# One-core hybrid streaming step with expert retrieval: 88 instead of 72 score blocks ahead in layer 0, 94 instead of 82 in layer 1, the sample's second chain from block 40, own slots for the additions' index

## The chip, the cores and the metric

The kernel runs on one core of a Trainium2 chip. The metric is the device time of one execution in microseconds; lower is better. Three runs of the kernel before took 3999.14, 4004.71 and 4008.16 us, so the median is 4004.71 us. All times in the profile count from the start of its span.

## The reference

Two layers run over 512 prompt tokens (one stream) and 128 sample tokens (8 streams of 16) with shared weights and a model width of 1024. Layer 0's mixer is a gated convolution beside sliding-window attention, layer 1's is a gated linear recurrence in blocks of 16 tokens. After each mixer stands the expert retrieval, which is the bulk of the work:

```python
q = (xb @ w_query).reshape(TB, 8, 2, 128)            # 8 heads, two halves
s = einsum('thpd,hpkd->thpk', q, keys)               # 128 keys for each half
sv, si = top_k(s, 16)
cand = sv[:, :, 0, :, None] + sv[:, :, 1, None, :]   # 16 x 16 pairs
cv, ci = top_k(cand, 16);  gate = softmax(cv)        # 16 of 16384 experts a head
act = gelu(einsum('thkd,td->thk', u_tab[idx], xb))
y = einsum('thk,thkd->td', gate * act, v_tab[idx])   # u_tab, v_tab: 16384 x 1024
```

Everything is float32; the products are made of two float32r parts of each factor, so a product takes three matmuls.

## The kernel before, in words

Tokens are worked in tiles of 128: four of the prompt, one of the sample. The retrieval is done in two ways.

*By gathers* (`sparse_peer`, L852): for the sample's tile and the prompt's first tile, in both layers. For each of 128 chosen experts a token, POOL issues an indirect load of one row of `u` per token (512 KB, L880), the vector engine multiplies and sums it (L884); then 128 rows of `v` in the same way (L913, summed by L920; in layer 0 for the sample L944, summed on TensorE by L962). The six buffers `g` are shared, so a gather is issued when the vector engine is through with the sixth before it.

*Densely* (`dense_peer`, L974): the prompt's tiles 1 to 3 meet all 16384 experts, in 128 blocks of 128. A block takes a load of `uT`, its split in two parts by ScalarE (L240) and the vector engine (L241), 24 matmuls of scores, a gelu, a multiplication by the gates of that block (L1110), a second split, a load and split of `v`, and 18 matmuls into the accumulators (`combine`, L1122). The gates come from a table in DRAM (`gd`) that `found` builds tile by tile from one-hot products. In layer 1 the first of these tiles gets its gates otherwise: `spread` (L1052) adds each token's gates into a cleared table `gz` by 128 indirect DMAs, in groups of 16 with a fence (`stone`, L1063) between; the first fence also waits for the DMAs that clear `gz` (L180).

Scores don't need the gates. So the last NA of the 128 are scored ahead (`ahead`, L985): FIRST of them while the query projections run (`route_p`), EACH more in each step of `found`, the rest behind it. Their scores go to DRAM (`sd`, L997) and come back in the loop (`ge<-sd`). `FE = (FIRST, EACH, NA)` is (12, 5, 72) in layer 0 and (12, 8, 82) in layer 1. So the loop computes scores for the first 56 blocks in layer 0 and the first 46 in layer 1.

The sample's path is a chain of its own (`chain_s`): mixer, query projections, choice, and then its gathers, which are appended to the list `gathers`. Its layer 0 chain runs beside the prompt's mixer; its layer 1 chain is started within layer 0's dense loop at block `K0`, one step a block. `gather(n)` takes n steps of the first entry of `gathers`; the numbers GM, GR, GS and PACE say how many at each step of the mixer, the projections, the gates' stretch and the dense loop. In layer 0's loop it is called only if the first tile's gathers are at the head or the sample's chain isn't done.

The program text doesn't fix the order of the instructions. A scheduler of the tile framework orders each engine's list by priorities (the place in the text, plus 1000 for gathers in layer 0, in the mixers and in the gates' stretch) and by its own estimate of when operands are ready. Engines then run their lists strictly in that order, and SP and POOL issue their DMAs in theirs. `after` and `follow` add order-only edges.

Buffers: `ai` (5) holds the transposed choices of `found` and in layer 1 the index of `spread`; `gatea` (2) holds the gates of the dense tiles.

## Time and profile before

| | |
|---|---|
| Median of 3 runs | 4004.71 us |
| Profiled execution, its own time | 4018.61 us |
| Its span | 4016.7 us, mean granted clock 0.94 |
| TensorE busy (weight loads) | 3567.8 us, 89% (2921.1, 73%) |
| Vector engine busy | 3217.4 us, 80% |
| ScalarE, POOL busy | 1655.5 and 1596.2 us |
| DMA | 1097.66 MB, mean 273 GB/s |
| Largest shares of the chain of waits | L1122 on TensorE 10%, L1070 on POOL 5%, loads `ge<-sd` 4%, `gu<-u` 3% |

The stages, by the first and last instruction of each: mixer of layer 0 to about 420, query projections to 656, gates' stretch to 1116, dense loop 1116 to 2094, mixer of layer 1 to about 2620, projections and gates' stretch to 3271.7, dense loop to 4005. Busy shares are averages over these, and the stages have different limits; what a change in one of them is worth is read from that stage. PE is TensorE's matmuls, PEld its weight loads, DVE the vector engine, ACT ScalarE. The granted clock is a share of TensorE's upper level; a matmul at the lower level takes longer and so counts as more busy time.

### The profile page before, as it was taken

To read this page: it belongs to the slowest core of one execution; us is meant where nothing else is said; L and a number is where in the kernel's file an instruction comes from. 1 tells how busy PE (TensorE), PEld (TensorE's weight loads), DVE (VectorE), ACT (ScalarE), POOL (GpSimd) and SP (SyncE) were. 2 spreads that over 40 slices of the span, in tenths; PEclk is the share of its full clock that TensorE was granted. 3 is DMA by queue.
4 is the path that set the end of the run, shared out by engine and by line. 5 is a ranking of instruction groups with operands and counts; after the bars stand their busy time and mean duration, and the time that the engine had idled before them with its cause. 6 is when DMAs were issued, how large, how long until landed. Compare 5 with 4: busy or idle time off the path is not lost.

```text
span 4016.7 us, 51334 instructions
## 1 busy us (share of the span) xinstructions
PE 3567.8 (89%) x17676; PEld 2921.1 (73%) x17676; DVE 3217.4 (80%) x6206; ACT 1655.5 (41%) x2717; POOL 1596.2 (40%) x1173
## 2 busy tenths in 40 slices
PE   6978778999999999788998878787999949999998
PEld 4756666789779997556775555566999949998776
DVE  5558999886568879887679877899998738788898
ACT  6644222467633334334444333231348913333333
POOL 0001665431245555541003553564057764444443
PEclk8989899999999999999999777798999979999999
DMA  4334998886789999998665765688457769999999
GB/s 147 113 110 160 328 338 322 317 326 241 264 298 336 338 333 357 370 362 304 227 230 216 258 235 186 225 321 296 140 164 211 211 177 343 334 337 356 385 385 331
DMA packets 480134, 1097.66 MB, mean 273 GB/s; under 512 B 55537, under 2 KB 260337, under 8 KB 474737
## 3 DMA queue, kind: packets, MB, share of 16 engines
q1 hardware_dynamic: 313984, 557.38, 39.7%
q0 software_dynamic: 165888, 537.01, 37.9%
q8 instruction: 139, 2.28, 0.2%
q14 instruction: 123, 1.00, 0.1%
HBM read 1005.92 MB, written 89.23 MB: 273 GB/s over the span
## 4 chain that ended last, share of the span: by engine, by line
PE 22%; DVE 12%; DMA 10%; POOL 6%; issue 5%; ACT 1%; SPq 0%; DVEq 0%; POOLq 0%; ACTq 0%
PE py L1122 10%; POOL gz L1070 5%; DMA ge<-sd 4%; DMA gu<-u,idx 3%; PE ps L284 2%; DVE wlo L241 2%; DVE yv L920 2%; PE pb L284 2%; PE py L291 1%; PE py L292 1%; PE py L293 1%; DMA gz<-gatea,ati 1%; DVE gu L884 1%; PE ps L312 1%; DMA wraw<-v 1%
## 5 line engine op out<-in xcount | busy, mean ns | idle before, releaser
L240 ACT ACTIVATE whi<-wraw 128x1024 fp32r<-128x1024 f32 x710 | 741.3, 1054 | 1024.5 <-PE py L292 307.6
L241 DVE TENSOR_TENSOR wlo<-wraw,whi 128x1024 fp32r<-128x1024 f32 x710 | 862.0, 1217 | 315.1 <-ACT whi L240 124.9
L880 POOL DMA_INDIRECT gu<-u,idx x512 | 670.4, 1309 | 1028.5 <-DVE idx L874 380.1
L1122 PE MATMUL py<-whi,wt 128*128 128x512 f32 x3072 | 798.8, 405 | 107.4 <-ACT wt L240 90.6
L1122 PEld LDWEIGHTS py<-whi,wt 128*128 128x128 f32 x3072 | 581.5, 192 | 258.9 <-ACT wt L240 102.3
L913 POOL DMA_INDIRECT gv<-v,idx x384 | 522.0, 1359 | 540.6 <-DVE yv L920 357.0
L884 DVE CUSTOM_DVE_ANT_0 gu<-gu,xnn 128x1024 f32<-128x1024 f32 x512 | 616.2, 1218 | 58.2 <-DMA gu<-u,idx 57.0
L291 PE MATMUL py<-xhl,whi 128*128 128x512 f32 (+1 forms) x1344 | 522.5, 389 | 74.5 <-ACT xhl L240 30.8
L293 PE MATMUL py<-xhl,wlo 128*128 128x512 f32 (+1 forms) x1344 | 515.9, 385 | 26.6 <-DVE wlo L241 26.3
L292 PE MATMUL py<-xhl,whi 128*128 128x512 f32 (+1 forms) x1344 | 514.1, 382 | 11.1 <-DVE xhl L241 11.0
L920 DVE SCALAR_TENSOR_TENSOR yv<-gv,wact,yv 128x1024 f32<-128x1024 f32 x381 | 486.7, 1277 | 2.7
L1122 PE MATMUL py<-wlo,wt 128*128 128x512 f32 x1536 | 401.6, 393 | 0.7 <-DVE wlo L241 0.7
L291 PE MATMUL ps<-xhl,whi 128*128 128x384 f32 (+1 forms) x1120 | 387.2, 346 | 7.9 <-ACT sm L510 3.7
L293 PE MATMUL ps<-xhl,wlo 128*128 128x384 f32 (+1 forms) x1120 | 388.5, 347 | 3.6 <-DVE wlo L241 3.4
L292 PE MATMUL ps<-xhl,whi 128*128 128x384 f32 (+1 forms) x1120 | 385.1, 344 | 0.0
L291 PEld LDWEIGHTS py<-xhl,whi 128*128 128x128 f32 x1344 | 264.6, 197 | 133.7 <-ACT xhl L240 35.1
L1122 PEld LDWEIGHTS py<-wlo,wt 128*128 128x128 f32 x1536 | 288.6, 188 | 67.6 <-DVE wlo L241 1.3
L1070 POOL DMA_INDIRECT gz<-gatea,ati x128 | 249.2, 1947 | 202.6 <-DVE mr L771 162.1
L293 PEld LDWEIGHTS py<-xhl,wlo 128*128 128x128 f32 x1344 | 264.4, 197 | 84.9 <-DVE wlo L241 37.7
L292 PEld LDWEIGHTS py<-xhl,whi 128*128 128x128 f32 x1344 | 264.8, 197 | 46.8 <-DVE xhl L241 15.1
L944 POOL DMA_INDIRECT gv<-v,idt x128 | 151.7, 1185 | 324.5 <-PE pb L962 296.3
L291 PEld LDWEIGHTS ps<-xhl,whi 128*128 128x128 f32 x1120 | 213.9, 191 | 21.3 <-ACT ge L996 5.8
(444 smaller groups left out, 4947.0 us busy)
## 6 DMA issues: line engine op xcount, KB each, us to landing
wraw<-uT SPq DMA_DIRECT2D x256, 512.0 KB
wraw<-v SPq DMA_DIRECT2D x256, 512.0 KB
wraw<-w SPq DMA_DIRECT2D x98, 512.0 KB
gd<-st SPq DMA_DIRECT2D x40, 1024.0 KB
wraw<-wq SPq DMA_DIRECT2D x64, 512.0 KB
sd<-ge SPq DMA_DIRECT2D x154, 192.0 KB
gch<-gd SPq DMA_DIRECT2D x32, 768.0 KB
ge<-sd SPq DMA_DIRECT2D x114, 192.0 KB
```

The costliest lines, as they stand in the source:

```text
L240: S.activation(hi, src, AF.Copy)
L241: return V.tensor_tensor(lo, src, hi.bitcast(F32), op=OP.subtract)
L284: m = T.matmul(p, w[wv][:, k], xhl(xv, k), start=(k == 0 and xv == wv), stop=(k == 7 and wv == 1))
L291: T.matmul(p, w[0][:, k], xhl(0, k), start=(k == 0), stop=False)
L292: T.matmul(p, w[0][:, k], xhl(1, k), start=False, stop=False)
L293: T.matmul(p, w[1][:, k], xhl(0, k), start=False, stop=(k == 7))
L880: P.indirect_dma_start(out=rows[s], out_offset=None, in_=t["u"][l], in_offset=bass.IndirectOffsetOnAxis(ap=idx[:, s:s + 1], axis=0))
L884: d = V.tensor_tensor_reduce(out=g, in0=g, in1=xn, scale=1.0, scalar=0.0, op0=OP.mult, op1=OP.add, accum_out=w[:, s - LG:s - LG + 1])
L913: P.indirect_dma_start(out=rows[s], out_offset=None, in_=t["v"][l], in_offset=bass.IndirectOffsetOnAxis(ap=idx[:, s:s + 1], axis=0))
L920: d = V.scalar_tensor_tensor(y, rows[e], w[:, e:e + 1], y, op0=OP.mult, op1=OP.add)
L1070: d = P.indirect_dma_start(out=flat, out_offset=bass.IndirectOffsetOnAxis(ap=ati[:, j:j + 1], axis=0), in_=gate[:, j:j + 1], in_offset=Non ...
L1122: mult[1] = T.matmul(yp[a][hf], wt[:, wv, 128 * a:128 * a + 128], vh[vv][:, 512 * hf:512 * hf + 512], start=(k == 0 and wv == 0 and vv == ...
```

## The change

Layer 0: NA 72 to 88 and EACH 5 to 7 (with DEEP, the number of blocks at the start whose scores and weights alternate between two buffers, 54 to 38), the first tile's gathers are appended at step 6 of the gates' stretch (KQ) instead of at block 1 of the loop, the sample's layer 1 chain starts at block 40 instead of 56 (K0), and `gather` is called in the loop whenever there is anything to gather. Layer 1: NA 82 to 94 and EACH 8 to 10, and the step that contains `spread` is written ahead of the first tile's own choice (`sparse_peer`). Buffers: the index of `spread` gets slots of other tiles (`idf`, `bt`), `gatea` three buffers; the zero tile that clears `gz` is halved, so the clearing goes in pieces of 512 bytes instead of 1024.

```diff
--- before.py
+++ after.py
@@ -26,7 +26,7 @@
 KT = (1, 0)
 LATER = 1000
 ORDER = ('SSPSPSPSPSPPPPPPPPSPSPPPSPSPSPSS','SPPP'*50)
-K0, SN = 56, (1,)
+K0, SN = 40, (1,)
 PS = 1000
 SW2 = [('g', 'g', 'g')]
 SB2 = ['s']
@@ -40,13 +40,13 @@
 PO = (0, 1)
 PEO = (0, 1)
 LG = 4
-DEEP = (54, 126)
+DEEP = (38, 126)
 LW = (1000, 1000)
 RS = 0
 SUM = dict(s=(None, "xn"), t=("vm", "vm"))
-KQ = (-1, -1)
+KQ = (6, -1)
 SC = (0, 1)
-FE = ((12, 5, 72), (12, 8, 82))
+FE = ((12, 7, 88), (12, 10, 94))
 
 
 class Group:
@@ -71,7 +71,7 @@
 
     BUFS = {"u4": 2, "uh": 2, "lo": 2, "v4": 4, "vh": 2, "w3": 2, "ge": 2, "g8": 2,
             "nat": 2, "g": NG, "sq": 2, "at": 2, "ai": 5, "vm": 1, "bt": 2, "bi": 2, "el": 2, "els": 2, "ln": 1,
-            "gatea": 2, "mr": 1, "xa": 2, "xb": 4}
+            "gatea": 3, "mr": 1, "xa": 2, "xb": 4}
 
     def tl(tag, shape, dt=F32, name=None):
         return sb.tile(shape, dt, name=name or tag, tag=tag, bufs=BUFS.get(tag, 1))
@@ -166,7 +166,7 @@
                         op0=OP.is_ge, op1=OP.mult)
         V.tensor_tensor(place[:, 0:1], place[:, 0:1], place[:, 1:2], op=OP.add)
     gz = dr.tile([4, 128, 128, 32], F32, name="gz", tag="gz", bufs=1)
-    zero = con.tile([128, 256], F32, name="zero")
+    zero = con.tile([128, 128], F32, name="zero")
     stone = con.tile([1, 1], F32, name="stone")
     fills = []
 
@@ -175,9 +175,9 @@
         while mark[0] is None:
             yield 1
         after(V.memset(zero, 0.0))
-        flat = gz.rearrange("g p k t -> (g p k t)").rearrange("(p r c) -> p r c", p=128, c=256)
-        for i in range(0, 64, 16):
-            fills.append(Y.dma_start(flat[:, i:i + 16], zero[:, None].to_broadcast([128, 16, 256])))
+        flat = gz.rearrange("g p k t -> (g p k t)").rearrange("(p r c) -> p r c", p=128, c=128)
+        for i in range(0, 128, 32):
+            fills.append(Y.dma_start(flat[:, i:i + 32], zero[:, None].to_broadcast([128, 32, 128])))
             for _ in range(6):
                 yield 1
 
@@ -1052,10 +1052,10 @@
         def spread(k1, k2, gate):
 
 
-            at = tl("ai", [128, 128], name="at0")
+            at = tl("idf", [128, 128], name="at0")
             V.scalar_tensor_tensor(at, k2, 128.0, k1, op0=OP.mult, op1=OP.add)
             V.tensor_scalar(at, at, 32.0, place[:, 0:1], op0=OP.mult, op1=OP.add)
-            ati = tl("ai", [128, 128], I32, name="ati")
+            ati = tl("bt", [128, 128], I32, name="ati")
             V.tensor_copy(ati, at)
             flat = gz.rearrange("g p k (t o) -> (g p k t) o", o=1)
             last = fills
@@ -1246,11 +1246,14 @@
             if i < FE[l][0]:
                 next(de)
             gather(GR[l])
+        if SC[l]:
+            next(de)
+            gather(GS[l])
         spt = sparse_peer(GT, l, xt, sv[:, 0], si[:, 0], "v4", SUM["t"][l])
         next(spt)
         if KT[l] < 0:
             gathers.append(spt)
-        for i in range(12 - 4 * SC[l]):
+        for i in range(12 - 5 * SC[l]):
             next(de)
             if i == KQ[l]:
                 gathers.append(spt)
@@ -1263,9 +1266,9 @@
             tg["s"] = dict(w=[SW1], sq="sq", r="pa", v="pb", a="idf", x="pa")
             cs = chain_s(1)
         for k, _ in enumerate(de):
-            if k == KT[l]:
+            if k == KT[l] and KQ[l] < 0:
                 gathers.append(spt)
-            if l or gathers and (gathers[0] is spt or cs is not None):
+            if gathers:
                 gather(PACE[l][k % len(PACE[l])])
             if l == 0 and cs is not None and k >= K0:
                 if spt not in gathers:
```

Three places of the engines' lists.

The vector engine in layer 1's mixer, before, at the end of a unit's state updates. L652 is a state update, L884 a gather's multiply and sum (its second row reads the sum out):

```order
L675 MEMSET s_in 128x128
L652 SCALAR_TENSOR_TENSOR s_in<-s_in,el,ps 128x128 x2
L652 SCALAR_TENSOR_TENSOR s_in<-s_in,el,py_18163 128x128 x2
L652 SCALAR_TENSOR_TENSOR s_in<-s_in,el,py_18167 128x128
L884 ISA gu,wact<-gu,xnn 128x1024
L884 ISA wact 128x1
L652 SCALAR_TENSOR_TENSOR s_end<-s_in,el,py_18167 128x128
L884 ISA gu,wact<-gu,xnn 128x1024
L884 ISA wact 128x1
```

And now, some way further on in the same mixer (L920 is the sum over gathered rows of `v`):

```order
L920 SCALAR_TENSOR_TENSOR yv<-gv,wact,yv 128x1024
L652 SCALAR_TENSOR_TENSOR s_in<-s_in,el,ps 128x128
L920 SCALAR_TENSOR_TENSOR yv<-gv,wact,yv 128x1024
L652 SCALAR_TENSOR_TENSOR s_in<-s_in,el,ps 128x128
L920 SCALAR_TENSOR_TENSOR yv<-gv,wact,yv 128x1024
L652 SCALAR_TENSOR_TENSOR s_in<-s_in,el,py_18768 128x128
L920 SCALAR_TENSOR_TENSOR yv<-gv,wact,yv 128x1024
L652 SCALAR_TENSOR_TENSOR s_in<-s_in,el,py_18768 128x128
L920 SCALAR_TENSOR_TENSOR yv<-gv,wact,yv 128x1024
L652 SCALAR_TENSOR_TENSOR s_in<-s_in,el,py_18772 128x128
```

Before, two gather steps stood among six updates; now one stands between any two, and the sample's `v` gathers, which had stood in the mixer's end and in the projections, are here.

SP before, at the end of layer 1's gates' stretch. `wraw<-uT` loads a block's weights, `sd<-ge` stores its scores ahead, `gd<-st` stores gates, `gch` reads them back, from `gz` those that were added:

```order
L997 DMA sd<-ge 128x384
L272 DMA wraw<-uT 128x1024
L997 DMA sd<-ge 128x384
L272 DMA wraw<-uT 128x1024
L1049 DMA gd<-st_25503 128x2048
L1049 DMA gd<-st_25504 128x2048
L272 DMA wraw<-uT 128x1024
L1105 DMA gch<-gz 128x4x128
L1107 DMA gch<-gd 128x8x128
L272 DMA wraw<-v 128x1024
L1105 DMA gch<-gz 128x4x128
```

And now:

```order
L1049 DMA gd<-st_26027 128x2048
L1049 DMA gd<-st_26028 128x2048
L997 DMA sd<-ge 128x384
L272 DMA wraw<-uT 128x1024
L1105 DMA gch<-gz 128x4x128
L1107 DMA gch<-gd 128x8x128
L997 DMA sd<-ge 128x384
L1105 DMA gch<-gz 128x4x128
L272 DMA wraw<-uT 128x1024
L1107 DMA gch<-gd 128x8x128
L997 DMA sd<-ge 128x384
```

Before, all loads and stores of the blocks ahead stood in front of the first read from `gz`; now ten blocks' stores and their loads stand behind it.

The vector engine at the end of the program, before. L1149 adds the dense result to the tokens, L901 the gathered one:

```order
L1110 TENSOR_TENSOR ge<-ge,gch 128x384
L920 SCALAR_TENSOR_TENSOR yv<-gv,wact,yv 128x1024 x2
L241 TENSOR_TENSOR wlo<-wraw,whi 128x1024
L241 TENSOR_TENSOR wt<-ge,wt 128x384
L920 SCALAR_TENSOR_TENSOR yv<-gv,wact,yv 128x1024 x2
L241 TENSOR_TENSOR wlo<-wraw,whi 128x1024
L920 SCALAR_TENSOR_TENSOR yv<-gv,wact,yv 128x1024 x4
L901 TENSOR_TENSOR xp<-xp,pb 128x4x128
L1149 TENSOR_TENSOR xp<-xp,py_32293 128x4x128
L1149 TENSOR_TENSOR xp<-xp,py_32302 128x4x128
L901 TENSOR_TENSOR xp<-xp,pb 128x4x128
```

And now:

```order
L920 SCALAR_TENSOR_TENSOR yv<-gv,wact,yv 128x1024 x5
L1149 TENSOR_TENSOR xp<-xp,py_32377 128x4x128
L1149 TENSOR_TENSOR xp<-xp,py_32386 128x4x128
L920 SCALAR_TENSOR_TENSOR yv<-gv,wact,yv 128x1024
L1149 TENSOR_TENSOR xp<-xp,py_32395 128x4x128
L1149 TENSOR_TENSOR xp<-xp,py_32404 128x4x128
L1149 TENSOR_TENSOR xp<-xp,py_32413 128x4x128
L920 SCALAR_TENSOR_TENSOR yv<-gv,wact,yv 128x1024
L1149 TENSOR_TENSOR xp<-xp,py_32422 128x4x128
L920 SCALAR_TENSOR_TENSOR yv<-gv,wact,yv 128x1024 x12
L901 TENSOR_TENSOR xp<-xp,pb 128x4x128 x2
```

Before, eight gather steps stood behind the last multiplication L1110, all ahead of the dense result; now nineteen do, twelve of them behind the dense result.

## Rows read from the trace of the kernel before

**Rows 1.** Windows by stage: length, PE PEld DVE ACT POOL busy, clock, DMA, GB/s.
```profile
800.00:1088.00 288.00, 288.00 (x1839) 248.06 (x1839) 195.41 (x451) 199.66 (x433) 63.10 (x53) 1.00 0.74 273
...
1116.00:1584.00 468.00, 461.47 (x2302) 413.66 (x2302) 374.28 (x521) 170.42 (x234) 234.94 (x167) 0.99 0.93 332
1584.00:1855.00 271.00, 219.78 (x934) 161.40 (x935) 240.80 (x275) 110.03 (x144) 127.77 (x89) 0.93 1.00 360
1855.00:2094.00 239.00, 226.91 (x996) 175.55 (x995) 162.85 (x345) 98.77 (x143) 0.00 (x0) 0.99 0.69 229
2094.00:2139.00 45.00, 32.96 (x143) 23.59 (x142) 42.52 (x145) 25.20 (x37) 0.09 (x1) 0.89 0.60 212
2139.00:2503.00 364.00, 295.37 (x1431) 203.77 (x1430) 295.31 (x583) 117.43 (x146) 170.09 (x134) 0.81 0.68 235
2503.00:2620.00 117.00, 95.44 (x459) 65.56 (x457) 104.35 (x155) 31.30 (x41) 55.68 (x41) 0.81 0.66 225
2620.00:2790.00 170.00, 135.01 (x584) 110.90 (x584) 162.72 (x309) 45.76 (x59) 101.82 (x81) 0.90 0.91 329
...
2952.00:3218.00 266.00, 262.36 (x1666) 259.60 (x1664) 215.81 (x292) 208.87 (x500) 213.18 (x111) 0.99 0.72 201
3218.00:3271.70 53.70, 0.18 (x2) 0.00 (x0) 2.37 (x4) 1.99 (x4) 36.76 (x26) 0.54 0.28 29
3271.70:3655.00 383.30, 383.27 (x1897) 344.23 (x1898) 306.08 (x452) 137.45 (x183) 174.92 (x138) 0.99 0.94 337
3655.00:4005.00 350.00, 338.14 (x1440) 268.33 (x1438) 316.38 (x357) 123.01 (x157) 163.40 (x119) 1.00 1.02 377
```

**Rows 2.** Chain that ended last, layer 1's dense loop: start us, us, what.
```profile
3600.67 4.18 PE ps L284 x24
3604.85 4.18 PE py L1122 x18
```

**Rows 3.** Windows, line L1122 (combines) alone, layer 0's last two stretches.
```profile
1584.00:1855.00 271.00, 159.07 (x576) 115.72 (x576) 0.93 1.00 360
1855.00:2094.00 239.00, 182.98 (x720) 133.76 (x720) 0.99 0.69 229
```

**Rows 4.** Windows, line L884 alone, between scans of layer 1's mixer.
```profile
2156.70:2220.40 63.70, 34.09 (x56) 0.91 0.85 311
2220.40:2286.60 66.20, 35.32 (x58) 0.73 0.80 275
2286.60:2336.20 49.60, 20.81 (x34) 0.96 0.66 221
2336.20:2401.10 64.90, 29.33 (x48) 0.71 0.68 230
2401.10:2465.00 63.90, 29.24 (x48) 0.71 0.69 234
2465.00:2503.10 38.10, 7.35 (x12) 0.91 0.43 144
```

**Rows 5.** Windows, line L920 alone, mixer's end and route.
```profile
2503.00:2620.00 117.00, 51.93 (x41) 0.81 0.66 225
2620.00:2790.00 170.00, 103.56 (x83) 0.90 0.91 329
```

**Rows 6.** Waits, 3210 to 3280: total us, times, longest.
```profile
DVE ge L1110 <- DMA gch<-gd: 51.1, 1, 51.1
```

**Rows 7.** Line L1070: duration ns min/median/max, first and last start.
```profile
L1070 POOL DMA_INDIRECT gz<-gatea,ati x128: 1546/1941/8077, 2952.2 to 3261.9; - x128
```

**Rows 8.** Timeline of POOL: start us, us, engine, line, [idle before].
```profile
2991.85 0.09 POOL L1063 MEMSET stone<- 1x1 f32 x1 [2.48 <-DMA gz<-gatea,ati]
...
3199.35 0.09 POOL L1063 MEMSET stone<- 1x1 f32 x1 [2.85 <-DMA gz<-gatea,ati]
```

**Rows 9.** Timeline of the vector engine at the end.
```profile
3992.12 0.55 DVE L1110 TENSOR_TENSOR ge<-ge,gch 128x384 f32<-128x384 f32 x1
...
4000.35 5.24 DVE L920 SCALAR_TENSOR_TENSOR yv<-gv,wact,yv 128x1024 f32<-128x1024 f32 x4
```


## The prediction

> **What bounds the kernel now.** I read the busy time by stage first: a stage in which TensorE is busy all the time gets longer by what is put into it, one in which it idles may not. Then the chain of waits for the price of a block, the vector engine's gather steps between landmarks of the recurrent mixer, and the waits around the start of layer 1's dense loop. "A gather" is one 512 KB indirect load by POOL with the vector step (L884 or L920) that uses it up.
>
> Four regimes [rows 1]. (1) Layer 0's gates stretch (800 to 1088) and the first 56 blocks of its dense loop (1116 to 1584): TensorE busy 288.0 of 288 and 461.5 of 468 us at the full clock, so it bounds. (2) Blocks 56 to 88 (1584 to 1855): TensorE 219.8 of 271, but the DMA share is 1.00 at 360 GB/s and the vector engine is busy 240.8; gathers and weights bound. (3) The recurrent mixer (2139 to 2503): TensorE and vector engine both busy 295 of 364, TensorE at a granted clock of 0.81, a part of the time at the lower of its two levels, so its busy time is stretched; here each gather delays the vector engine's own order. (4) Layer 1's gates stretch (2952 to 3218) is TensorE's, then a hole of 53.7 us with 0.18 busy, then a dense loop bound by TensorE (383.3 of 383.3) and at its end by DMA (377 GB/s) as well.
>
> A block's scores are 24 matmuls, 4.18 us, and its combine is 18 matmuls, 4.18 us [rows 2].
>
> **The change part by part.** The sum is made against the profiled execution, span 4016.7 us (4018.6 with what lies around it, 13.9 above the median 4004.7).
>
> (a) *16 more blocks scored ahead in layer 0.* 16 x 4.18 = 66.9 us more TensorE work in a stretch where it is busy 288 of 288 [rows 1, 2]: +67. Their weight loads and stores lie beside it (DMA share 0.74). Bounds 55 (a part of it fills TensorE's pause between 1088 and the first combine at 1116) and 70.
>
> (b) *Layer 0's loop.* Before: 56 blocks in 468 us (8.36 each, scores and combine), 32 in 271 (8.47), 40 in 239 [rows 1, 3]. In the new order blocks 40 to 88 hold what 56 to 88 held: one weight of the sample's chain and about three gathers per block; the gathers end at block 88 in both orders. The pace of the gathers there is set by DMA, so I take 8.47 for all 48: 40 x 8.36 = 334, 48 x 8.47 = 407. So the sixteen scores taken out of blocks 40 to 56 give nothing back; the cover they had was the gathers'. In the last 40 blocks TensorE has 226.9 - 183.0 = 43.9 us of other work [rows 1, 3]; of the chain's 134 wide matmuls there, 60 stay, so -20: 219. Sum 960 against 978: -18. Bounds: -95 if the 48 blocks ran at TensorE's own 219.8/32 = 6.87 us, 0 if the tail kept its length.
>
> The start of the first tile's gathers "from mid gates' stretch" doesn't happen in the order: the sample's gathers stand ahead of it on POOL, and the vector engine's first step for this tile stays behind block 0's multiplication, with 128 sample steps before it in both orders. Price 0.
>
> (c) *Between the loops* (2094 to 2139). The sample's last choices leave the vector engine (42.5 busy of 45 there), 21 gathers take their place (21 x 1.22 = 26 us). POOL now has 23 gathers ahead of the fence that waits for DRAM's clearing, 105 behind it; the clearing has half the packet size. Taken at 0, bounds -10 and +15.
>
> (d) *The mixer.* Because the sample's chain ends within layer 0's loop, its gathers are written earlier and the scheduler packs them denser: between the third and the tenth scan (L574; 2139 to 2503) stand 222 gathers, before 128. Between two scans, a gather counting twice: 28 gathers 63.7 us, 29 66.2, 17 49.6, 24 64.9, 24 63.9, 6 38.1 [rows 4]. From 6 to 29 that is (66.2 - 38.1)/23 = 1.22 us each, and the vector engine's own time for one is 35.32/29 = 1.22 us. 94 more: +115 by this slope. Floor: the vector engine's 295.3 us plus 94 x 1.22 = 410, +46, if its idle time swallows what it can. From 24 to 29 gathers the time hardly rose, so I take +90.
>
> (e) *What those gathers leave.* From 2503 to 2790 stood 41 + 83 gathers [rows 5]; 3 remain. TensorE idles 57 of 287 us there (95.4 + 135.0 busy), so at most that goes while its clock stays as it is: -57. Bounds: -88 at the full clock all through (95.4 x 0.81 + 135.0 x 0.90 = 199 us of work), -30 if half the idle is latency of normalisation and recurrence.
>
> (f) *Layer 1's gates stretch.* Twelve more blocks ahead, 50 us, go into the hole. It was one wait for the first chunk of gates [rows 6] behind the 128 additions [rows 7]. These now start ahead of the first tile's own choice. Ahead loads left when they start: about 67, before 45, so TensorE needs 67 x 4.18 plus the gates' own 266 - 45 x 4.18 = 78: 358 us. The additions under load take 207.5/5 = 41.5 us for sixteen [rows 8], 8 x 41.5 = 332. But on SP the first read of the added gates now stands ahead of ten of the ahead blocks, so it is reached at about 358 - 45 = 313 and holds SP for some 20 us, with two loads in flight. Hole -53.7, work +50.2, first chunk and splits +7, SP's stall about +8: +12. Bounds 0 and +35. The own slots for the index and the third gate buffer: nothing in this stretch was seen waiting for one, 0.
>
> (g) *Layer 1's loop.* 12 x 4.18 = -50. But its gathers keep the pace of 12 per 8 blocks, so more are left over: 8 stood behind the last multiplication, now 19. The vector engine takes 5.24/4 = 1.31 us for one at the end [rows 9]; with POOL's issue up to 1.9. 11 x 1.5 = +17. Together -33, bounds -45 and -15.
>
> The Trainium skill ("DMA: Bandwidth & Descriptors", Specifications) gives a core about 358 GB/s of HBM. By that limit the loop's 383.3 x 337 + 350 x 377 = 261 MB, less 12 x (0.52 - 0.20) = 257, need 718 us against 733, so (g) would be -15. The trace moved 377 GB/s for 350 us [rows 1], so I don't take it as a limit.
>
> Sum: 67 - 18 + 0 + 90 - 57 + 12 - 33 = +61 us, 1.5%. On the median: 4004.7 + 61 = 4066 us.
>
> **The rivals.**
> *Faster: the mixer's idle time swallows the gathers.* Its vector engine idles 69 of 364 us; if the denser order fills that, (d) is +46, and if TensorE behind it runs at the full clock, (e) is -88: 67 - 18 + 46 - 88 + 12 - 33 = -14, 3991 us. It decides where (d) + (e) falls below -36. For: 24 and 29 gathers take the same time. Against: the slope over the whole range equals the engine's own price, and each unit is a chain through TensorE and back. Chance 0.12.
> *Blocks 40 to 88 are not the gathers'.* With DMA less loaded they would run at the vector engine's 240.8/32 = 7.5 us: -46 more, +15, 4020; at TensorE's 6.87: -77 more, 3989. Against: share 1.00, and the same mix again. Chance 0.08.
> *Everything linear and the additions late.* (d) +115, (f) +35: +109, 4114. For: the slope, and the wait of 51 us that these additions made before [rows 6]. Chance 0.10.
> *The page's 358 GB/s* for (g): +79, 4084; the row speaks against it; within the forecast's range.
>
> **How the numbers follow.** Forecast +61 with 0.70; its own range, with (b), (d), (e) and (f) off by 10 to 30 each, +20 to +100. The range to 4000 leaves out the faster cases, to 4112 most of the linear one. This kernel's runs can tell 0.2%, 8 us. Slower by more: 0.70 + 0.10 and a part of the second rival, 0.79; within: 0.06; faster: 0.12 and the rest of the second rival, 0.15.
>
> **What would show it.** (a) block 0's first combine about 67 us later; (b) eight blocks still take 66 to 68 us from 40 to 88, and layer 0's loop ends some 50 us later than 2094; (d) third to tenth scan about 454 us; (e) scan ten to the last route choice shorter by about 57, without gathers; (f) no hole of 50 us, SP's wait on the additions under 40; (g) a loop of 700 us with more than ten gather steps in a row at the very end, TensorE done. Wrong if the mixer takes under 420 us, or if blocks 40 to 56 run at less than 7.5 us.

## The result, and the profile after

The changed kernel takes 4040.1 us (median of 4 runs, 4039.0 to 4042.9), the kernel before 4005.7 beside it: ratio 1.0078, 95% interval 1.0063 to 1.0093, so 34 us slower. The forecast was +61 (4066, range 4000 to 4112). Direction and range held; its two largest terms did not, as the stages show.

Stages of the changed kernel (length, then PE, PEld, DVE, ACT, POOL busy, clock, DMA share, GB/s), against [rows 1]:

```profile
840.00:1140.00 300.00, 300.00 (x1885) 272.58 (x1885) 176.83 (x350) 193.92 (x404) 45.08 (x32) 1.00 0.67 242
1140.00:1167.80 27.80, 14.96 (x69) 6.54 (x67) 4.43 (x10) 4.23 (x8) 9.36 (x10) 0.80 1.04 393
1167.80:1508.50 340.70, 334.29 (x1666) 294.03 (x1666) 265.78 (x393) 121.27 (x168) 164.50 (x124) 0.99 0.92 332
1508.50:1926.30 417.80, 335.74 (x1398) 253.39 (x1399) 366.02 (x472) 166.35 (x228) 184.02 (x137) 0.89 0.98 351
1926.30:2143.80 217.50, 204.51 (x853) 157.98 (x852) 176.97 (x415) 74.23 (x96) 28.09 (x19) 0.97 0.74 247
2143.80:2199.60 55.80, 36.20 (x118) 22.25 (x116) 39.19 (x64) 23.33 (x34) 20.87 (x18) 0.82 0.96 324
2199.60:2608.90 409.30, 315.54 (x1436) 214.42 (x1436) 390.90 (x638) 119.42 (x148) 288.48 (x221) 0.76 0.91 326
2608.90:2876.70 267.80, 249.18 (x1263) 202.32 (x1264) 180.08 (x603) 86.02 (x115) 0.00 (x0) 0.92 0.25 86
...
3240.00:3318.90 78.90, 73.07 (x420) 72.25 (x419) 23.75 (x22) 33.79 (x53) 24.45 (x15) 0.96 0.64 195
...
3600.00:4006.60 406.60, 391.75 (x1659) 309.68 (x1659) 363.09 (x443) 141.71 (x185) 185.94 (x140) 1.00 1.03 381
4006.60:4037.80 31.20, 5.80 (x34) 4.04 (x32) 23.16 (x23) 2.61 (x5) 11.73 (x10) 0.61 0.77 269
```

The rows run from layer 0's gates stretch through its loop (blocks 0 to 40, 40 to 88, 88 to 128) to the third scan, the tenth scan, the route's end, and on to layer 1's loop and the tail. The route's end is taken, here and in all that follows, at the start of the 56th of the route's 64 choices; the last one starts 14 to 20 us later in every trace (by it, (e) below would be -84.4 and (f) +25.8, their sum the same). The vector engine is busy 390.9 of the mixer's 409.3 us, before 295.3 of 364.0; behind the tenth scan three gather steps are left (DMA share 0.25).

The terms of the sum, in the two profiled executions:

```
term                                       forecast   measured
(a) gates stretch, to block 0's combine      +67      +51.5  (1116.3 -> 1167.8)
(b) layer 0's loop                           -18       -1.5  (977.4 -> 975.9)
(c) loop's end to third scan                   0      +10.7  (45.1 -> 55.8)
(d) third to tenth scan                      +90      +45.1  (364.2 -> 409.3)
(e) tenth scan to the route's end            -57      -79.8  (347.6 -> 267.8)
(f) to layer 1's loop                        +12      +21.2  (421.0 -> 442.2)
(g) layer 1's loop and tail                  -33      -26.1  (733.0+11.9 -> 687.7+31.2)
sum                                          +61      +21.1
```

The spans differ by 21 and the medians by 34: the profiled execution of before, 4018.6, lies in the upper part of its runs. The stages tell where time went; the verdict is the medians'.

The hole of [rows 6] is gone and the additions of [rows 7] stayed as slow. SP's waits and the additions' line of the changed kernel:

```profile
SPq L1105 <- DMA gz<-gatea,ati: 8.8, 1, 8.8
```

```profile
L1070 POOL DMA_INDIRECT gz<-gatea,ati x128: 1545/1959/7975, 2939.8 to 3266.8; - x128
```

They start 63 us behind the route's end, before 101 us, but take 327 us for 310, and 52 us pass from the last one to the first combine (before 10), in which TensorE works off the scores that SP loads behind that read: it is busy 73.1 of the 78.9 us from 3240 on.

The end, vector engine and then TensorE, against [rows 9]:

```profile
4000.43 6.55 DVE L920 SCALAR_TENSOR_TENSOR yv<-gv,wact,yv 128x1024 f32<-128x1024 f32 x5
...
4013.46 7.88 DVE L920 SCALAR_TENSOR_TENSOR yv<-gv,wact,yv 128x1024 f32<-128x1024 f32 x6
4022.35 2.63 DVE L920 SCALAR_TENSOR_TENSOR yv<-gv,wact,yv 128x1024 f32<-128x1024 f32 x2 [1.01 <-DMA gv<-v,idx]
```

```profile
4030.88 1.11 PE L929 MATMUL pb<-ident,yv 128*128 128x128 f32 x4 [20.14 <-DVE yv L920]
```

TensorE waits 20 us for the gather steps left over: the tail of (g), +19.3 for the forecast's +17.

### The profile page after: what moved, and what is told of

It is laid out like the page before. It is cut to its first block, busy times and chain, and to the rows that moved or that the text cites. A ratio compares the mean times of both kernels' runs of the same rounds, so it can differ in the third digit from the quotient of the medians.

```text
span 4037.8 us, 51523 instructions
## 1 busy us (share of the span) xinstructions
PE 3586.7 (89%) x17676; PEld 2935.1 (73%) x17676; DVE 3216.5 (80%) x6206; ACT 1655.6 (41%) x2718; POOL 1596.6 (40%) x1173
## 5 line engine op out<-in xcount | busy, mean ns | idle before, releaser
L1122 PE MATMUL py<-whi,wt 128*128 128x512 f32 x3072 | 814.8, 411 | 88.3 <-ACT wt L240 83.1
L1122 PEld LDWEIGHTS py<-whi,wt 128*128 128x128 f32 x3072 | 590.5, 195 | 250.8 <-ACT wt L240 100.4
L913 POOL DMA_INDIRECT gv<-v,idx x384 | 503.4, 1311 | 466.0 <-DVE yv L920 329.5
L884 DVE CUSTOM_DVE_ANT_0 gu<-gu,xnn 128x1024 f32<-128x1024 f32 x512 | 615.7, 1216 | 33.0 <-DMA gu<-u,idx 32.4
L291 PE MATMUL py<-xhl,whi 128*128 128x512 f32 (+1 forms) x1456 | 556.5, 383 | 69.3 <-ACT xhl L240 29.1
L293 PE MATMUL py<-xhl,wlo 128*128 128x512 f32 (+1 forms) x1456 | 554.7, 382 | 27.8 <-DVE wlo L241 27.5
L292 PE MATMUL py<-xhl,whi 128*128 128x512 f32 (+1 forms) x1456 | 549.2, 377 | 9.5 <-DVE xhl L241 9.5
L920 DVE SCALAR_TENSOR_TENSOR yv<-gv,wact,yv 128x1024 f32<-128x1024 f32 x381 | 488.2, 1281 | 4.9 <-DMA gv<-v,idx 2.4
L1070 POOL DMA_INDIRECT gz<-gatea,ati x128 | 264.9, 2070 | 375.1 <-DVE mr L771 334.5
L1122 PE MATMUL py<-wlo,wt 128*128 128x512 f32 x1536 | 399.3, 393 | 0.0
L291 PE MATMUL ps<-xhl,whi 128*128 128x384 f32 (+1 forms) x1104 | 382.3, 346 | 13.4 <-ACT whi L240 7.5
L292 PE MATMUL ps<-xhl,whi 128*128 128x384 f32 (+1 forms) x1104 | 378.1, 343 | 0.0
L291 PEld LDWEIGHTS py<-xhl,whi 128*128 128x128 f32 x1456 | 284.8, 196 | 124.3 <-ACT xhl L240 33.3
L293 PEld LDWEIGHTS py<-xhl,wlo 128*128 128x128 f32 x1456 | 284.3, 195 | 84.8 <-DVE wlo L241 38.5
L1122 PEld LDWEIGHTS py<-wlo,wt 128*128 128x128 f32 x1536 | 289.9, 189 | 65.7
L292 PEld LDWEIGHTS py<-xhl,whi 128*128 128x128 f32 x1456 | 284.7, 196 | 44.1 <-DVE xhl L241 13.1
```

The source lines that it names most:

```text
L291: T.matmul(p, w[0][:, k], xhl(0, k), start=(k == 0), stop=False)
L292: T.matmul(p, w[0][:, k], xhl(1, k), start=False, stop=False)
L293: T.matmul(p, w[1][:, k], xhl(0, k), start=False, stop=(k == 7))
L884: d = V.tensor_tensor_reduce(out=g, in0=g, in1=xn, scale=1.0, scalar=0.0, op0=OP.mult, op1=OP.add, accum_out=w[:, s - LG:s - LG + 1])
L913: P.indirect_dma_start(out=rows[s], out_offset=None, in_=t["v"][l], in_offset=bass.IndirectOffsetOnAxis(ap=idx[:, s:s + 1], axis=0))
L920: d = V.scalar_tensor_tensor(y, rows[e], w[:, e:e + 1], y, op0=OP.mult, op1=OP.add)
```

## The experiments

Twelve kernels ran, each timed beside the kernel before. What parts they hold and their stages, read from each trace. "3rd" is the third scan; the numbers in brackets are gathers ahead of it, from there to the tenth scan, and behind that:

```
run               block 0  loop 0  ->3rd  3rd->10th  ->route's end  (gathers)    ->loop 1  loop 1  tail   ratio
before             1116.3   977.4   45.1    364.2      347.6   (0/128/128)         421.0   733.0  11.9
after              1167.8   975.9   55.8    409.3      267.8   (31/222/3)          442.2   687.7  31.2  1.0078
e1_layer1_only     1114.4   977.6   45.1    370.0      341.8   (0/128/128)         443.9   686.9  30.9  0.9992
e2_layer0_only     1168.1   972.5   56.3    410.9      267.3   (31/222/3)          431.6   740.3  11.3  1.0141
e5_before_dense    1111.3   976.6   45.1    427.7      300.1   (0/220/36)          426.1   740.5  11.3  1.0114
e8_layer1_dense    1113.7   979.7   45.2    429.3      299.8   (0/220/36)          441.9   687.2  31.4  1.0047
e3_sample_late     1170.2   973.4   47.4    360.8      346.9   (17/111/128)        432.5   687.4  30.8  1.0108
e4_k0_56           1172.1   961.8   44.2    428.2      300.4   (0/220/36)          441.7   687.8  31.1  1.0155
e10_88_ahead       1115.6   978.2   45.1    364.6      347.8   (0/128/128)         438.2   718.7  11.8  1.0013
e11_88_sparse      1113.4   981.6   45.1    339.3      390.3   (0/102/154)         431.3   723.3  11.7  1.0062
e12_slow_gathers   1112.0   956.5  111.1    362.6      349.4   (17/110/129)        414.9   733.3  12.0  1.0135
e13_layer1_slow    1115.2   957.7  113.7    332.1      337.5   (24/112/120)        441.7   687.0  31.2  1.0010
e14_front_loaded   1117.6   978.5   45.3    347.4      369.6   (0/123/133)         437.6   688.6  31.2  1.0019
e15_64_ahead       1099.3   976.8   47.3    410.5      344.6   (0/128/128)         414.5   731.8  12.0  1.0091
```

My theory after reading the trace was *idle*: the denser gathers cost only the vector engine's busy floor and give back more behind it, so layer 0's 16 blocks are the loss. The rival was *slope*, the forecast's own: each gather put into the mixer costs its 1.22 us. A difference between two of these kernels is uncertain by the intervals of both, some 8 to 12 us.

**Layer 1's part alone** (e1): the kernel before with the additions' slots, the third gate buffer, the two steps at the route's end, the half-size clearing, and

```diff
-FE = ((12, 5, 72), (12, 8, 82))
+FE = ((12, 5, 72), (12, 10, 94))
```

> Only the part of the change that belongs to layer 1 (94 blocks scored ahead, own slots for the additions, third gate buffer, the two steps before the route's end); layer 0 and the recurrent mixer's gathers as before. My forecast's terms (f) + (g) give +12 - 33 = -21, 3985 us. The two traces read together (gates stretch +21, loop -45, tail +19) give -5, 4001 us. A third reading, that the whole loss sits here, needs +34, 4040 us. In the trace: loop of layer 1 about 45 us shorter than before, 19 gather steps behind the last multiplication, tail about 31 us.

Measured 4007.0 against 4009.2, ratio 0.9992 (0.9980 to 1.0005): no change. By stage +22.9 (to the loop), -46.1, +19.0, what the change shows in (f) and (g). The reading of the two traces holds; the forecast's -21 fails by (f) and the tail.

**Layer 0's part alone** (e2): the layer 0 numbers below, `KQ`, the new condition and the half-size clearing; the index in its shared slot, two gate buffers.

```diff
-K0, SN = 56, (1,)      DEEP = (54, 126)   FE = ((12, 5, 72), ...
+K0, SN = 40, (1,)      DEEP = (38, 126)   FE = ((12, 7, 88), ...
```

> Only the part that belongs to layer 0 (88 blocks scored ahead, the sample's chain from block 40, the first tile's gathers queued earlier, clearing in half-size packets); the index stays in its shared slot, two gate buffers, layer 1's dense part as before. The mixer's gathers are the dense ones (222 between the third and the tenth scan). My forecast's terms (a) to (e) give 67 - 18 + 0 + 90 - 57 = +82, 4088 us. The two traces read together give 51.5 - 1.5 + 10.7 + 45.1 - 79.8 = +26, 4032 us; with the parts adding up to the measured 34 and -5 for the other half, +39, 4045.

Ratio 1.0141 (1.0120 to 1.0162), +56 us. Stages (a) to (e) repeat the changed kernel within 4 us; the rest is behind them: the old layer 1 part takes 431.6 and 740.3 us here for 421.0 and 733.0. So the whole loss belongs to layer 0's part, as both theories said, and layer 1's part is worth 22 to 25 us behind dense gathers (after against e2, e8 against e5) and 2 behind the old ones. What makes this difference I did not settle.

**Dense gathers alone** (e5), on the kernel before, and **with layer 1's part** (e8):

```diff
-GM, GR, GS = ((4,),(1,)*40+(2,)*60), (8,8), (8,8)
+GM, GR, GS = ((4,),(3,)), (8,8), (8,8)
```

> The kernel before with nothing changed but the gathers per step of layer 1's mixer, one list replaced by a constant three: layer 0 is untouched, and between the third and the tenth scan stand 220 gathers for 128. Theory idle (the vector engine's idle time takes most of the gathers in, and what they leave behind is worth more): mixer +44 (busy floor 295.3 + 92 x 1.22 = 407.5 against 364), stretch to the last route choice -80, sum -36, 3970 us. Theory slope (as I forecast): +88 - 57 = +31, 4037 us.

> Layer 1's part of the change and the dense gathers in the mixer, layer 0 as before. Theory idle: -36 - 5 = -41, 3965 us, so faster than both kernels. Theory slope: +31 - 21 = +10, 4016 us.

Ratios 1.0114 (1.0096 to 1.0132) and 1.0047 (1.0030 to 1.0064): +46 and +19 us where *idle* expected -36 and -41. That theory falls. Third scan to the route's end grew from 711.8 to 727.8 (e5) and from 711.7 to 729.0 us (e8 against e1): 92 more gathers cost 59 to 64 us in front of the tenth scan and give back 42 to 48 behind it. (The profiled execution of e5, 4040.7 us, is its fastest, 13 us under its median, so its stages show 22 of the 46 us.) Yet the changed kernel takes 677 us there. What it has and these two have not is 31 gathers ahead of the third scan, and the sample's last choice is out of its mixer (9.6 us less on lines L837, L840 and L841 there).

**The changed kernel with the sample's gathers held back** (e3) and **with its chain from block 56** (e4):

```diff
-            if gathers:
+            if l or gathers and (gathers[0] is spt or cs is not None):
```

```diff
-K0, SN = 40, (1,)
+K0, SN = 56, (1,)
```

> The changed kernel with the old condition in the dense loop (sample's gathers not begun inside layer 0's loop): 17 instead of 31 gathers before the third scan, 111 instead of 222 between the third and the tenth, 128 instead of 3 behind it; everything else as changed. Theory packing (dense gathers in the mixer cost more than they give back; the run that adds them to layer 1's part was 22 us slower than that part alone): 4040 - 22 = 4018 us. Theory shift (what gains is each gather moved out of the stretch from the third scan to the last route choice, 0.64 us each by 347.6 - 267.8 us for 125 gathers): that stretch 712 - 17 x 0.64 = 701 us against 677, less some 8 us of gathers ahead of the third scan: 4056 us.

> The changed kernel with the sample's chain of the next layer begun at block 56 as before, not at block 40, so that blocks 40 to 56 hold neither scores nor chain. Theory gathers (their DMA sets the pace of blocks 40 to 88 whatever TensorE does): blocks 40 to 56 keep 8.7 us each; the chain ends later (last 40 blocks 239 for 217), the order has no gathers ahead of the third scan (-11), third scan to last route choice as in the dense run on the old layer 0, 729 for 677: 4040 + 21 - 11 + 52 = 4102 us. Rival (the chain's matmuls and weights pace them): 16 blocks at 6.87 us instead of 8.7, 29 us less, 4073 us.

e3: 4051.2 us, ratio 1.0108 (1.0086 to 1.0130), where *shift* said 4056 and *packing* 4018: with the chain early, starting the sample's gathers in the loop gains 11 us (707.7 to 677.1 us from the third scan to the route's end, less 8 ahead of it and 10 behind), at the edge of what the two intervals can tell, though a like order without the early chain lost 22 (e1 to e8). e4: 4070.8, ratio 1.0155 (1.0129 to 1.0180), where the rival said 4073. Its windows for blocks 40 to 56 and 56 to 88:

```profile
1512.00:1648.10 136.10, 112.45 (x412) 83.14 (x412) 122.22 (x158) 56.49 (x74) 64.89 (x48) 0.88 1.01 362
1648.10:1901.00 252.90, 195.77 (x856) 148.85 (x857) 213.44 (x241) 87.08 (x115) 122.05 (x89) 0.89 0.98 355
```

But the edit did not empty blocks 40 to 56. The scheduler put the chain's first products (L312) there all the same, 108 of them with 16 loads of their weights, as in the changed kernel. Windows of L312 alone (TensorE busy, weight loads busy, clock, DMA share, GB/s), of e4, of before, and of the changed kernel:

```profile
1512.00:1648.10 136.10, 34.51 (x108) 22.23 (x108) 0.88 1.01 362
1648.10:1901.00 252.90, 25.64 (x90) 16.53 (x90) 0.89 0.98 355
```

```profile
1584.00:1855.00 271.00, 55.01 (x192) 35.15 (x192) 0.93 1.00 360
```

```profile
1508.50:1645.90 137.40, 34.52 (x108) 22.36 (x108) 0.88 1.00 358
1645.90:1926.30 280.40, 51.77 (x180) 34.52 (x180) 0.89 0.97 347
```

So the 136.1 us, 8.5 a block, for 137.4 compare like with like and decide nothing between theory and rival; that the rival's sum came out is luck. What the edit moved is the rest of the chain, whose last product now stands at 2127.5 us (changed kernel 2000.9). Blocks 56 to 88 hold 90 of its products here, 192 before and 180 in the changed kernel, with 89 gathers in all three, and take 252.9 us for 271.0 and 280.4. DMA moved 89.7 MB in them for 97.5 and 97.2, at a share of 0.97 to 1.00. So these blocks go by the bytes that DMA moves, the chain's weights as well as the gathers'; what blocks with neither scores nor chain would take stays open.

e4 and e8 have nearly the same gathers in each unit and differ by the 16 blocks ahead, and with them by the chain's start: gates stretch +58.4, loop -17.9, together 4070.8 for 4029.5, +41 us. That is the loss. The chain's earlier end earns 31 of it back (e4 to after), in the last 40 blocks (-15.5) and from the third scan on (-51.5), less 28.8 in blocks 40 to 88 and 11.6 behind the loop.

**88 blocks ahead in layer 1** (e10: e1 with `(12, 9, 88)`) and **sparse gathers on it** (e11: `GM` of layer 1 all ones).

> Layer 1's part alone, with 88 blocks scored ahead in layer 1 instead of 94 (82 before). The order leaves 9 gather steps behind the last multiplication, with 94 it left 19, before 8. If the tail is what eats the loop's gain (11.9 to 31 us), the tail falls to about 14 us, the loop grows by 6 x 4.18 = 25, the gates stretch shrinks by 25: 17 us under that part with 94, 3988 us. If the gates stretch is held by the additions (its hole returns) it does not shrink: 4013 us.

> As the run with 88 blocks scored ahead in layer 1, and in layer 1's mixer one gather per step throughout instead of one, later two: 102 gathers between the third and the tenth scan for 128, 26 more behind it. If packing costs linearly (24 us for 92 gathers): 7 us under that run. If gathers cost the same in either place: equal. If the tenth scan onwards is the dearer place (0.64 us each and nothing gained in front): +17.

e10: ratio 1.0013 (0.9999 to 1.0026), 4018.3: the tail fell to 11.8 as expected, the loop grew by 31.8, the stretch shrank by 6. The hole is back:

```profile
3200.00:3237.00 37.00, 13.91 (x78) 13.04 (x76) 2.45 (x2) 2.99 (x4) 27.90 (x19) 0.76 0.36 64
3237.00:3290.00 53.00, 39.87 (x219) 39.28 (x220) 14.65 (x15) 17.29 (x24) 2.36 (x3) 0.84 0.59 186
```

TensorE has 13.9 us of work in 37 while POOL ends the additions: they hold the stretch, and blocks ahead only fill it. e11: ratio 1.0062 (1.0041 to 1.0083), +17 us on e10, the third reading to the microsecond (729.6 for 712.4 from the third scan on). So fewer gathers in the mixer cost as much as more: of the splits tried with this layer 0 (102, 123, 128 and 220 ahead of the tenth scan), 128 is the best.

**Gathers slower in layer 0's loop** (e12: one number on the kernel before), and **the same with layer 1's part and the new condition** (e13).

```diff
-PACE = ((4,4,4,0)*10+(4,)*90,(3,))
+PACE = ((4,4,4,0)*10+(2,)*90,(3,))
```

> The kernel before with one number changed: from block 40 of layer 0's dense loop on, at most two gathers per block instead of four. In the order, blocks 56 to 88 then hold 67 gathers for 95, blocks 88 to 128 hold 52 for none, 17 of the sample's stand ahead of the third scan for none. Theory gathers (they and their DMA hold blocks 56 to 88 at 8.47 us, TensorE has 6.87 of work there): 56 to 88 shorter by up to 51 us; 88 to 128, where TensorE was busy 227 of 239, longer by 10 to 30 (the vector engine 163 + 52 x 1.22 = 226); third scan to last route choice about 4 us shorter: 3965 to 3990 us. Theory total (what is taken out of one stretch comes back in the next, as the two are one pool of DMA and vector work): 56 to 88 -30, 88 to 128 +30, 4007 us.

> As the run with two gathers per block from block 40 of layer 0, with layer 1's part of the change and the new condition in the dense loop (sample's gathers begun in it): 24 of the sample's gathers ahead of the third scan, 112 from there to the tenth, 120 behind it. If layer 1's part and the shift add to it (-2 for the part, 7 more gathers ahead at 1.6 us each = -11): 13 us under that run. If neither does: equal.

e12: ratio 1.0135 (1.0120 to 1.0151); both theories miss. Blocks 56 to 88, and the stretch from the loop's end to the third scan:

```profile
1578.00:1806.80 228.80, 201.02 (x865) 152.39 (x865) 198.64 (x238) 104.66 (x136) 113.41 (x65) 0.96 0.99 348
...
2068.50:2179.60 111.10, 56.28 (x154) 29.68 (x153) 91.77 (x241) 24.34 (x35) 27.54 (x23) 0.68 0.68 238
```

The blocks run at 7.15 us instead of 8.47, with 65 gathers for 89 and 79.7 MB for 97.5, so the gathers' bytes did hold them. The loop gets only 21 us shorter, and the sample's chain now stands among gathers in the last 40 blocks: the stretch behind the loop takes 66 us more, with 84 us of vector work besides gathers in it for 50 before. The room in those blocks was the chain's. e13 gets 42 us back from the third scan to the route's end and ends at 1.0010 (1.0001 to 1.0019), 49 us under e12, where I expected 13 or none. Nearly all of it is the vector engine's wait for gathered rows in the mixer, e12 and then e13:

```profile
DVE gu L884 <- DMA gu<-u,idx: 80.0, 50, 4.3
```

```profile
DVE gu L884 <- DMA gu<-u,idx: 38.7, 28, 3.8
```

With 110 and 112 gathers there its busy time is the same, 269 and 267 us. Why the rows came later in e12 was not settled.

**Gathers at the mixer's front** (e14: e1 with `GM` of layer 1 `(3,)*30+(0,)*70`).

> Layer 1's part alone (layer 0 as before), and in layer 1's mixer three gathers per step for the first 30 steps, then none: between the scans from the fourth on stand 30, 42, 32, 6, 7, 6 gathers, where the kernel before has 28, 29, 17, 24, 24, 6; 133 behind the tenth. Theory step: a unit between two scans takes 38 to 39 us with 6 to 8 gathers (granted clock above 0.9), 48 to 52 with 11 to 17, 62 to 66 with 20 to 33 (clock 0.71 to 0.8), 72 with 42; so 66 + 72 + 64 + 38.5 + 38.5 + 38.5 = 317 us for 346 before, 29 less; with 5 more gathers behind the tenth scan at 0.5 to 1.7 us (+3 to +8): 21 to 26 us under layer 1's part alone, 3982 us. Theory linear (1.22 us for each gather, or about 0.7 by the dense runs, wherever it stands): 123 gathers for 128, -4 to -6, and as much back behind the tenth scan: 4005 us.

Ratio 1.0019 (1.0003 to 1.0035), 4015.3: neither. The units behaved nearly as *step* said: 71.6, 70.6, 39.9, 44.2, 38.7 us for 42, 32, 6, 7, 6 gathers, and the mixer is 17 to 23 us shorter than before and than e1. But behind the tenth scan it is 22 to 28 us longer with five more gathers. Up to the route's first choice it took 137 us with 29 gathers (e1 156 with 62), from there 232 with 104 (e1 186 with 66): 1.2 us for each more among the choices, which are the vector engine's own work.

**Fewer blocks ahead in layer 0** (e15: 64 for 72, chain from block 64, on the kernel before).

> The kernel before with layer 0's numbers moved the other way: 64 blocks scored ahead in layer 0 for 72 (the change has 88), the sample's chain from block 64 for 56; layer 1's numbers as before. Theory ahead (a block scored ahead costs its 4.18 us in the gates stretch and gives little back in the loop, whose blocks 40 to 88 the gathers hold): gates -33 or -26 by the change's 51.5/16, loop about 0, the sample's end up to +10: 3975 to 3990 us. Theory chain (the sample's chain is as long as the room it has, so its later start of 8 blocks comes out behind the loop): gates -26, loop to third scan +30 or more, the last 40 blocks +8 (as the run with block 56 for 40, +15.5 for 16): 4010 to 4025 us.

Ratio 1.0091 (1.0075 to 1.0108), worse than either theory. The gates stretch gave back 17 us and the third scan came 15.5 us earlier, but the unit behind the fourth scan took 94.2 us with 16 gathers, before 63.7 with 28. Groups of the vector engine in it:

```profile
L840 DVE TENSOR_TENSOR oh<-oh,tops 128x1024 f32<-128x1024 f32 x4 | 4.9, 1224 | 0.1
L837 DVE TENSOR_TENSOR oh<-iu,iota 128x1024 f32<-128x1024 uint32 x4 | 4.9, 1222 | 0.1
L841 DVE TENSOR_REDUCE kf<-oh 128x64 f32<-128x1024 f32 x4 | 4.9, 1219 | 0.1
```

Those are steps of the sample's last choice, which before ended ahead of the fourth scan but for one; the gathers that need it started behind it. So the chain's end came out one stretch later than I had looked for it. Its gain in layer 0 was lost there. Blocks and chain were moved together here, so what eight blocks fewer are worth by themselves stays open. Nothing that ran beats the kernel before; layer 1's part alone equals it.

## Why the prediction was right, and where it was not

**(a) 16 blocks, +67 forecast, +51.5 measured**; over all runs the first combine comes at 1169.6 with 88 blocks (four runs) and 1114.4 with 72 (nine), +55, the lower bound. My reason for that bound was wrong: TensorE's pause is still there (15.0 busy of 27.8). Other work was pushed behind block 0. Line L962 up to that point, before and after:

```profile
L962 PE MATMUL pb<-gv,zr 128*32 128x512 f32 x508 | 104.9, 621 | 12.2 <-DMA gv<-v,idt 11.1 <-DVE zr L955 1.1
```

```profile
L962 PE MATMUL pb<-gv,zr 128*32 128x512 f32 x472 | 91.5, 609 | 5.2 <-DMA gv<-v,idt 3.5 <-DVE zr L955 1.1 <-DVE sv L772 0.5
```

36 of its products, 13.4 us, left the stretch; blocks 0 to 40 then took 340.7 us for the forecast's 334.

**(b) Layer 0's loop, -18 forecast, -1.5.** That DMA sets the pace of blocks 40 to 88 was the right reading (e12: 7.15 us a block with fewer gathers; e4: 7.9 with as many gathers and less of the chain), and the last 40 blocks came out as forecast (217.5 for 219). But the pace isn't the gathers' alone, as the prediction has it. The 48 blocks took 417.8 for 407: the same 3.05 MB a block, at 351 GB/s instead of 360. The loop's end, 50 us later, was called.

**(c) 0 forecast, +10.7**, inside its bounds, with 17 of POOL's gathers and 16 of the vector engine's steps in it, where the prediction had 21; 15 more steps stand at the loop's end. I priced them there at nothing, which was about right, and did not see what they are worth later.

**(d) and (e) are the step that failed: +33 forecast, -34.7 measured.** The prediction's own sign of being wrong came with them, a mixer under 420 us (409.3). I laid a line through [rows 4] from 6 gathers to 29, 1.22 us each, and lengthened it. The units follow it no further than some 20 gathers; then they lie flat. Units between two scans of before, of e13, and of the changed kernel:

```profile
2156.70:2220.40 63.70, 56.49 (x288) 39.24 (x287) 57.96 (x115) 22.08 (x28) 39.96 (x33) 0.91 0.85 311
...
2401.10:2465.00 63.90, 47.49 (x213) 32.56 (x212) 49.11 (x100) 17.50 (x22) 33.39 (x26) 0.71 0.69 234
2465.00:2503.10 38.10, 33.66 (x200) 23.42 (x199) 26.89 (x62) 15.80 (x21) 7.36 (x6) 0.91 0.43 144
```

```profile
2377.90:2442.00 64.10, 42.10 (x203) 28.61 (x204) 47.63 (x97) 16.91 (x21) 31.04 (x24) 0.72 0.68 225
2442.00:2480.90 38.90, 35.65 (x214) 25.34 (x212) 27.94 (x65) 15.08 (x20) 9.11 (x8) 0.93 0.52 167
```

```profile
2288.70:2362.00 73.30, 53.41 (x228) 35.64 (x227) 69.39 (x139) 16.96 (x22) 54.71 (x44) 0.71 0.93 337
2362.00:2424.60 62.60, 46.32 (x214) 30.98 (x213) 60.19 (x94) 17.97 (x23) 45.08 (x35) 0.74 0.91 326
...
2551.00:2608.90 57.90, 42.80 (x206) 28.05 (x204) 56.58 (x81) 15.72 (x21) 38.29 (x30) 0.75 0.90 321
```

Units with 6 to 9 gathers take 38 to 44 us, with 11 to 13 48 to 51, with 15 to 17 50 to 60 (e15's 94.2 apart). From 20 to 34 gathers all units of all runs took 55 to 67 us (one 70.6); 37, 42 and 45 took 69.6, 71.8 and 75.9 (e8), 0.8 us for each more. Four of before's six units already stood on the flat part, so the denser order put most of its gathers where they cost little.

What was filled there is the vector engine's wait for rows that have not landed. That wait in the whole mixer, before and in the changed kernel:

```profile
DVE gu L884 <- DMA gu<-u,idx: 46.8, 31, 3.6
```

```profile
DVE gu L884 <- DMA gu<-u,idx: 4.1, 6, 2.4
DVE yv L920 <- DMA gv<-v,idx: 0.8, 4, 0.2
```

The engine's busy time rose by 95.6 us and its idle time fell by 50, from 68.7 to 18.4: together the +45. That was my first rival, its +46 for (d) and nearly its -88 for (e); (d) + (e), -34.7, stopped 1.3 us short of the -36 at which it was to decide. For (e) I had counted TensorE's idle time, 57 us, but the stretch had been the vector engine's:

```profile
2503.10:2850.70 347.60, 286.60 (x1337) 226.97 (x1336) 325.20 (x729) 93.04 (x121) 157.61 (x122) 0.88 0.72 255
```

It was busy 325.2 of 347.6 us. In the changed kernel it is busy 180.1 of 267.8, and TensorE 249.2.

Idle time filled isn't enough by itself: 92 more without the early start lost 16 us on balance (e5, e8). The changed kernel's (d) + (e) take 677 us, e8's 729, 20 of the difference in (d) and 32 in (e). How much of it the 31 gathers ahead of the third scan are worth was argued and not shown: with 17 ahead e3 took 707.7 and e12 712.0 us, with 24 e13 669.6.

The granted clock does not by itself set a unit's length. Most units from 20 gathers on have a mean of 0.68 to 0.85, between TensorE's two levels, 1.2 and 2.4 GHz, and those with 6 to 9 gathers 0.86 to 0.97; but before's first unit above took 63.7 us at 0.91, with more matmuls. What goes with the clock is TensorE's idle time: about a tenth of the time in this unit and in the short ones, a quarter to a third in the others shown. The Trainium skill ("TensorE: Matmul & The Clock Gate", HAM oscillation) tells of loops whose pauses bring the clock down, so that the next piece of work starts slow. The rows agree in kind: the units at a low clock are those with pauses. No run here parts what the clock takes from what the pauses take. What sets the length of a unit in between is open too: 17 gathers took 59.2 us in e12 and 51.9 in e13.

**(f) +12 forecast, +21.2**, inside its bounds. The additions were priced 332 us and took 327; what I mis-sized is the work behind SP's read, 52 us from the last addition to the first combine.

**(g) -33 forecast, -26.1**, by its own mechanism: loop -45.3 for -50, tail +19.3 for +17. The 358 GB/s for each core that the Trainium skill states ("DMA: Bandwidth & Descriptors", Specifications), which would have made (g) -15, did not bind: the trace has 381 GB/s over 406.6 us. The same page of the Trainium skill gives that figure, under Measured, as each core's share with both cores of an HBM domain streaming; one core runs here.

**Where the 34 us come from**, by the ratios in a row: layer 1's part -3, the dense order +22, 16 blocks ahead with the chain's start +43, the chain's earlier end -31, +31 together, each of the last three to some 8 to 12 us (the parts depend on their order: behind the early chain the dense order gains 11). So the forecast was right in sign because of (a), which gave little back, and near in size by luck, because its misses had both signs: 68 us too much for (d) and (e) and 15.5 for (a), 43 too little for (b), (c), (f) and (g), 61 - 68 - 15.5 + 43 = 21 in the profiled executions.

## What to carry to other kernels

Before a slope is drawn through a table of stretches, look whether its upper end lies flat: four of six units had the same length with 24 to 29 gathers. Then look what the engine that is to pay does in them: in units of 24 gathers the vector engine stood 13 to 15 us waiting for rows, and that was room. Work that fills waits has to go somewhere, so price a move by both stretches, the one that it enters and the one that it leaves, and by what else had been using that room: the loop's last 40 blocks had belonged to the sample's chain. Scoring 16 more blocks ahead took TensorE's work out of blocks that DMA then held at the same length (blocks 40 to 56: 134.5 us before, 137.4 now) and put it into a stretch that TensorE holds; that was a loss of some 41 us here.

## What the runs showed of the hardware

- One core's 16 DMA engines moved 381 GB/s for 407 us, gathers and weights mixed (after).
- A unit in which TensorE idled 16 of 64 us had a granted clock of 0.71, one in which it idled 22 of 64 had 0.72, and one in which it idled 7 of 64 had 0.91 (before, e13, before).
- Thirty-two blocks of layer 0's loop (56 to 88) took 271.0 us for 97.5 MB, 252.9 for 89.7 and 228.8 for 79.7 (before, e4, e12), at DMA shares of 0.98 to 1.00 and 348 to 360 GB/s.
- The vector engine waited 46.8 us for gathered rows in a mixer with 128 gathers, and 4.9 us in one with 222 (before, after).
- An addition into DRAM under load was not quicker for having its own index slot and an earlier start: 128 of them took 304 to 314 us in the five kernels with layer 1's old part, 317 to 328 in the nine with the new one, which also scores more blocks beside them.
